# When GpSimd computes the S5 layer's second set of phases: first of its tables, or behind the last split of the first norm's output

## The chip, the cores and the metric

The kernel runs on one core of a Trainium2 chip. The core has five engines that run side by side and wait for each other by semaphores: TensorE (PE in the rows below, its weight loads PEld), VectorE (DVE), ScalarE (ACT), GpSimd (POOL) and SyncE (SP, which here only issues DMAs; ACT and POOL issue DMAs too). Every engine runs its own instructions strictly in order, so an instruction that waits holds up all that stand behind it on its engine. The metric is device time in microseconds (us); less is better.

## The reference

One block of a hybrid model on 1024 tokens and 256 context tokens, 1024 wide, in fp32: a norm with modulation, one wide projection `w_in`, two token mixers (an S5 state space layer and a gated linear attention), and a mixture of 64 experts. What matters here is the start: the first norm, the first columns of the projection (`u`, the S5 input), and the tables that S5 needs.

```python
h = rms_norm(x, lp['norm1_g']) * (1.0 + sc1) + sh1
hc = rms_norm(ctx, lp['norm1_g']) * (1.0 + csc1) + csh1
z = h @ lp['w_in']
zc = hc @ lp['w_in']
...
lam_dt = lam * dt
b_bar = ((jnp.exp(lam_dt) - 1.0) / lam)[..., None] * b
...
a = jnp.broadcast_to(jnp.exp(lam_dt), bu.shape)
_, states = lax.associative_scan(_linear_recurrence_op, (a, bu), axis=1, reverse=reverse)
```

S5 runs forward (direction 0) and backward (direction 1), with 16 groups of 64 complex states each. The kernel works in chunks of 8 tokens. Its tables are powers of `exp(lam_dt)` times B (`wts`), times C (`ca`), their product (the kernel `kts`, stored to `kd`), and the *phases*: the unit complex numbers by which a state turns in 0 to 159 chunks, one table for each direction, stored to `phd`.

## The kernel before, in words

Every fp32 product on TensorE is made of three products of fp32r halves: a tile is split into a high part (ScalarE casts or adds the shift, `hH`, `hcH`, `wH`) and the rest (VectorE subtracts, `xl`, `xcl`, `wL`; lines 127 and 295). The first norm runs over three streams: the context (stream 0, 256 columns), and two halves of the tokens (streams 1 and 2, 512 columns each), 8 row blocks each. `stats` makes the sum of squares and the inverse root (`rsqrt`, lines 89 to 93: ScalarE's root, then four small VectorE instructions), `scaled` multiplies (line 284, one operand in PSUM), `split` makes high part and rest (lines 292 and 295). The first two weight tiles (`u`) are multiplied as the splits come, in `z_step`; then `values(0)` begins, the first of the projections for the attention, in tiles of 24 products, through three PSUM buffers `z`.

The first part is written out by hand, in `tc.manual_schedule()`: there each engine's instructions stand in the order of the code. Behind it a scheduler orders `s5_tables2`, `values(0)` and what is left of direction 0's phases.

`phases(d, X)` is a generator: it builds one direction's table on engine X by doubling. A first entry 1, a second entry from `ph`, and then eight rounds (1, 2, 4, ..., 64 and 31 columns wide for 8 groups) of one complex product each: six instructions a round, lines 1233 to 1248 (`cmul_steps`), each an elementwise product or sum of two tiles in SBUF. The table lies in the buffer `big0` or `big1`, and two DMAs of GpSimd's queue store it to `phd` (line 1316). Direction 0 runs on VectorE (`V`) and is drawn step by step by the hand-written order: 24 steps (four rounds) ahead of the norm's first `rsqrt`, 3 more later, and the rest behind the last split. Direction 1 runs on GpSimd (`G`), whole, when the tables begin. Behind it GpSimd makes `ca`: for each direction six products of 128x1152 elements, and two DMAs to `cad` (line 1328). Then come GpSimd's DMAs of the first S5 input tile (`u_out(0, G)`, line 313, 8 DMAs to `ud`).

`s5_tables2` uses the buffers `big0` and `big1` again: `kts` of block 0 lies in `big0`, that of block 1 in `big1`. ScalarE copies into it from PSUM (lines 1369 and 1370) and VectorE adds 16 columns (line 1371), so both must wait until that buffer's phases are stored. `wts` of direction 0 (VectorE; its real part is whole with line 1237) is transposed on TensorE (line 1348, PSUM tile `pt`), in the middle of `values(0)`. ScalarE empties the `z` buffers of `values(0)` (line 429, `vc` and `vt`); `vt` lies where the S5 input tiles were, and waits for the `ud` DMAs too.

Of the kernel before, what the change touches and what calls it, by code (L numbers as in the profile page):

```python
# [10 lines left out]
F32 = mybir.dt.float32  # L11
# [13 lines left out]
P = 128  # L25
# [18 lines left out]
def tile_kernel(ctx: ExitStack, tc: tile.TileContext, A: dict, dbg=None):  # L44
    nc = tc.nc
    V, S, G, PE = nc.vector, nc.scalar, nc.gpsimd, nc.tensor
# [34 lines left out]
    def mm3(out, lh, ll, rh, rl, start, stop):  # L81
        PE.matmul(out, lh, rh, start=start, stop=False)  # L82
        PE.matmul(out, lh, rl, start=False, stop=False)  # L83
        return PE.matmul(out, ll, rh, start=False, stop=stop)  # L84
# [19 lines left out]
    def half(dt=F32):  # L104

        return hp.tile([P, 512], dt, name="xl", bufs=2 * KD)

    def ctx_row(dt=F32):
        return hcp.tile([P, LC], dt, name="xcl", bufs=KD + 1)
# [42 lines left out]
    def z_half(H, L, n, out=None, ks=range(KD)):  # L152
        ps = zp.tile([P, 512], F32, name="z") if out is None else out
        for k in ks:
            ws = slice(k * P, k * P + P)
            ts = slice(n * 512, n * 512 + 512)
            lastmm[0] = mm3(ps, H[:, ws], L[:, ws], hH[:, k, ts], hL[n][k], k == 0, k == KD - 1)
        return ps
# [8 lines left out]
    with tc.manual_schedule(), tc.tile_pool(name="stp", bufs=1, space=PSUM) as qp, ExitStack() as small:  # L167
        q = small.enter_context(tc.tile_pool(name="st", bufs=1))
# [50 lines left out]
        def am_steps():  # L219
# [6 lines left out]
            )  # L226

        s5t = s5_tables(nc, tc, A, cad, phd, r8d, am_steps, *s5in)
        next(s5t)
        S.activation(lg, lg, AF.Exp)  # L230
# [50 lines left out]
        def scaled(r, k):  # L281
            rows_, _, lo, hi = streams[r]
            c = 1 if r == 0 else 0
            V.scalar_tensor_tensor(
                rows_[k], rows_[k], am[:, k, c : c + 1], prs[r][:, : hi - lo], ALU.mult, ALU.mult
            )

        def split(r, k):
            rows_, H, lo, hi = streams[r]
            c, ho = (1, 0) if r == 0 else (0, lo)  # L290
            xk, Hk, sh = rows_[k], H[:, k, ho : ho + hi - lo], mod[:, k, c : c + 1]
            S.activation(Hk, xk, AF.Identity, bias=sh)  # L292
            Lk = half(F32R) if r else ctx_row(F32R)
            (hL[r - 1] if r else hcL).append(Lk)
            return V.scalar_tensor_tensor(Lk, xk, sh, Hk.bitcast(F32), ALU.add, ALU.subtract).ins  # L295

        def some(g, n):
            for _ in range(n):
                next(g, None)
# [5 lines left out]
        def u_half(m, n, ps):  # L305
            for c in range(4):

                dst = us[m][:, :, 32:160].rearrange("p j (r c) -> p c j r", c=8)[:, n * 4 + c]
                V.tensor_copy(dst, ps.rearrange("p (c j r) -> p c j r", c=4, j=8)[:, c])

        def u_out(m, E):
            for j in range(8):
                E.dma_start(ud[m].rearrange("(j c) g k -> j g c k", j=8)[j], us[m][:, j])
            dump("us%d" % m, us[m])
# [7 lines left out]
        for g in (2, 3):  # L322
            some(md[g], 3)
        s5mid = next(s5t)
        some(s5mid[3], 24)
        some(st[0], KD + 1)
        some(st[1], 4)
        some(st[0], 1)
# [5 lines left out]
        some(md[0], 1)  # L334
        some(st[1], 1)
        scaled(0, KD - 1)
        some(s5mid[3], 3)
        some(st[1], 1)
        some(md[0], 2)
        for k in range(4):  # L340
# [42 lines left out]
        for k in range(KD + 1):  # L383
            if k < KD:
                scaled(2, k)
            if k in (2, 5):
                u_half(k // 5, 0, (z00, z10)[k // 5])
            if k:
                lastL = split(2, k - 1)
        u_half(0, 1, z_half(H0, L0, 1))  # L390
        u_out(0, G)
        u_half(1, 1, z_half(H1, L1, 1))
# [6 lines left out]


    with tc.issue_after(lastL):
        some(s5mid[3], 99)
    if stop_after <= 1:
        ws_.close(); s5s.close(); early.close(); zs.close(); fr.close()
        return
# [424 lines left out]
    q = xs_.enter_context(tc.tile_pool(name="wo", bufs=1, reuse_waits="tile"))  # L830
# [261 lines left out]
def s5_tables(nc, tc, A, cad, phd, r8d, more, q, qt, par, bt, ct):  # L1092
    V, S, G, PE = nc.vector, nc.scalar, nc.gpsimd, nc.tensor
# [131 lines left out]
    def cmul_steps(or_, oi, ar_, ai, br, bi, shp, E=V, own=None):  # L1225

        n_ = int(np.prod(shp))
        t = temp(E, n_, own)
        if len(shp) == 2:
            t = t.rearrange("p (a b) -> p a b", a=shp[0])  # L1230
        if len(shp) == 3:
            t = t.rearrange("p (a b c) -> p a b c", a=shp[0], b=shp[1])
        E.tensor_tensor(or_, ar_, br, ALU.mult)
        yield
        E.tensor_tensor(t, ai, bi, ALU.mult)
        yield
        E.tensor_tensor(or_, or_, t, ALU.subtract)
        yield
        E.tensor_tensor(oi, ar_, bi, ALU.mult)
        yield  # L1240
        t2 = temp(E, n_, own)
        if len(shp) == 2:
            t2 = t2.rearrange("p (a b) -> p a b", a=shp[0])
        if len(shp) == 3:
            t2 = t2.rearrange("p (a b c) -> p a b c", a=shp[0], b=shp[1])
        E.tensor_tensor(t2, ai, br, ALU.mult)
        yield
        E.tensor_tensor(oi, oi, t2, ALU.add)
        yield

    bb = q.tile([P, 2, 16, 16], F32, name="bb")
# [7 lines left out]
    pw = q.tile([P, 2, 9, 16], F32, name="pw")  # L1259
# [29 lines left out]
    dn = q.tile([P, 2, 9, 16], F32, name="dn")  # L1289
# [8 lines left out]
    ca = q.tile([P, 2, 2, 8, 144], F32, name="ca")  # L1298
    def phases(d, X):

        big = q.tile([P, 2560], F32, name=f"big{d}")
        pt_ = big.rearrange("p (r a k) -> p r a k", r=2, a=8)
        ds_ = slice(d * 8, d * 8 + 8)
        X.memset(pt_[:, 0, :, 0:1], 1.0)
        X.memset(pt_[:, 1, :, 0:1], 0.0)
        X.tensor_copy(pt_[:, 0, :, 1], ph[:, 0, ds_])
        X.tensor_scalar(pt_[:, 1, :, 1], ph[:, 1, ds_], 1.0 - 2.0 * d, None, ALU.mult)
        n_ = 1
        while n_ < 159:
            w_ = min(n_, 159 - n_)  # L1310
            bc = lambda r: pt_[:, r, :, n_ : n_ + 1].broadcast_to([P, 8, w_])
            yield from cmul_steps(pt_[:, 0, :, n_ + 1 : n_ + 1 + w_], pt_[:, 1, :, n_ + 1 : n_ + 1 + w_],
                 pt_[:, 0, :, 1 : 1 + w_], pt_[:, 1, :, 1 : 1 + w_], bc(0), bc(1), (8, w_), E=X)
            n_ *= 2
        for r in range(2):
            G.dma_start(phd[d, r], pt_[:, r])

    for _ in phases(1, G):
        pass
    for d in range(2):  # L1320
        ps_ = slice(d * 8, d * 8 + 8)
        pwd = (pw[:, 0], pwn) if d == 0 else (dn[:, 0], dnn)
# [3 lines left out]
        cmul(cv(0), cv(1), c_(0), c_(1), g(0), g(1), (8, 9, 16), E=G)  # L1326
        for r in range(2):
            G.dma_start(cad[d, r], ca[:, d, r])
    yield q, qt, cmul, phases(0, V), bb, ca, pw, dn


def s5_tables2(nc, tc, last, lastL, A, ident, kd, wtd, qp, q, qt, cmul, phases, bb, ca, pw, dn):
# [658 lines left out]
```

## Time and profile before

| | |
|---|---|
| median of 3 runs | 2132.8 us (2128.4 to 2133.94) |
| the profiled execution's own time | 2134.74 us |
| its span, first to last instruction | 2133.1 us |
| PE busy | 1979.8 us (93%) |
| DVE, ACT, POOL busy | 1295.5, 1003.6, 485.5 us (61, 47, 23%) |
| mean granted TensorE clock | 0.976 |

The profile is of one execution: for each instruction its engine, line, start and duration, and what ended the wait before it. A busy share is a mean over the whole program; the change touches its first 150 us, which have to be read by themselves.

### The profile page before, as it was taken

Reading aid. Unit: us, or ns where it says so; the run is one execution under the profiler, and the core shown is the slowest. Engines: PE = TensorE matmul, PEld = TensorE weight load, DVE = VectorE, ACT = ScalarE, POOL = GpSimd, SP = SyncE. Lnnn points to the kernel's source line nnn. Section 1 sums busy time; section 2 is a strip of 40 time slices with the busy share of each in tenths; the row PEclk is TensorE's granted clock in tenths of the full one; section 3 lists DMA queues with packets and bytes.
Section 4 is the critical chain, followed back from the end, with each engine's and each line's share of the span. In section 5 each row is a group of like instructions: output and inputs, shape, how many; then the busy total and the mean of one; then the engine's idle time right before and its main releaser. Section 6 shows DMA issues by size and latency. Waiting matters only on the chain. (4 is left out here: it accounts for less than half of the span.)

```text
span 2133.1 us, 30727 instructions
## 1 busy us (share of the span) xinstructions
PE 1979.8 (93%) x10313; PEld 1602.0 (75%) x10313; DVE 1295.5 (61%) x2123; ACT 1003.6 (47%) x1418; POOL 485.5 (23%) x399
## 2 busy tenths in 40 slices
PE   6789999999999999997999899899999999999983
PEld 2488889888777788885877688687888887777761
DVE  7864664664577644444558667756655657776736
ACT  4334454544532411112233456756565666766631
POOL 5510000000012000001101234333333334343322
PEclk8799999999999999998999999999999999999997
DMA  8251010101144344438432699888898889998966
GB/s 310 74 142 40 24 46 31 40 31 32 49 143 158 115 134 143 134 104 302 168 131 100 254 297 306 313 266 256 260 302 247 273 261 348 334 314 248 312 159 275
DMA packets 101516, 398.73 MB, mean 187 GB/s; under 512 B 14690, under 2 KB 21474, under 8 KB 79812
## 3 DMA queue, kind: packets, MB, share of 16 engines
q1 hardware_dynamic: 60576, 260.03, 34.3%
q0 software_dynamic: 31168, 117.81, 20.8%
q10 hardware_dynamic: 9572, 18.46, 2.4%
q8 instruction: 98, 1.61, 0.3%
q14 instruction: 102, 0.84, 0.1%
HBM read 456.25 MB, written 81.55 MB: 252 GB/s over the span
## 5 line engine op out<-in xcount | busy, mean ns | idle before, releaser
L1634 DVE TENSOR_TENSOR wl<-raw,wh 128x2048 fp32r<-128x2048 f32 x156 | 352.9, 2290 | 120.2 <-ACT wh L1628 119.1
L1687 PE MATMUL pa<-wh,xh 128*128 128x512 f32 x760 | 305.3, 402 | 0.0
L1688 PE MATMUL pa<-wl,xh 128*128 128x512 f32 x760 | 299.9, 395 | 1.2 <-DVE wl L1634 0.6
L1628 ACT CAST wh<-raw 128x2048 fp32r<-128x2048 f32 x156 | 292.7, 1916 | 0.1
L83 PE MATMUL z<-xl,wH 128*128 128x512 f32 x672 | 270.6, 403 | 8.9 <-DVE xl L295 8.9
L82 PE MATMUL z<-hH,wH 128*128 128x512 f32 x672 | 268.1, 399 | 2.7 <-ACT hH L292 1.6
L84 PE MATMUL z<-hH,wL 128*128 128x512 f32 x672 | 267.0, 397 | 0.0
L1690 PE MATMUL pa<-wh,xl 128*128 128x512 f32 x496 | 193.5, 390 | 0.0
L1687 PE MATMUL py<-wh,hh 128*128 128x512 f32 x380 | 159.0, 418 | 29.4 <-ACT y L1751 19.1
L1757 POOL DMA_INDIRECT acc<-y,si x62 | 98.3, 1586 | 346.3 <-ACT y L1751 206.5
L1688 PEld LDWEIGHTS pa<-wl,xh 128*128 128x128 f32 x760 | 143.5, 189 | 34.5 <-DVE wl L1634 8.0
L1687 PEld LDWEIGHTS pa<-wh,xh 128*128 128x128 f32 x760 | 143.7, 189 | 26.4
L83 PEld LDWEIGHTS z<-xl,wH 128*128 128x128 f32 x672 | 127.4, 190 | 35.6 <-DVE xl L295 12.5
L1688 PE MATMUL py<-wl,hh 128*128 128x512 f32 x380 | 152.8, 402 | 1.2 <-DVE wl L1634 1.2
L1690 PE MATMUL py<-wh,hl 128*128 128x512 f32 x380 | 150.9, 397 | 0.0
L127 DVE TENSOR_TENSOR wL<-wraw,wH 128x1024 fp32r<-128x1024 f32 x56 | 75.0, 1346 | 121.9 <-ACT wH L122 121.8
L82 PEld LDWEIGHTS z<-hH,wH 128*128 128x128 f32 x672 | 127.3, 189 | 27.9 <-ACT hH L292 1.8
L84 PEld LDWEIGHTS z<-hH,wL 128*128 128x128 f32 x672 | 127.6, 190 | 24.5 <-issue 0.7
L1646 POOL DMA_INDIRECT xg<-h2d,gi x63 | 119.7, 1900 | 51.5 <-DVE jk L1677 17.4
L122 ACT CAST wH<-wraw 128x1024 fp32r<-128x1024 f32 x56 | 58.8, 1050 | 148.3 <-PE z L83 65.0
L1718 ACT ACTIVATE sl<-pa 128x256 f32<-128x256 f32 x95 | 36.5, 384 | 191.3 <-DVEq L1715 119.9
L1666 ACT CAST xh<-pt 128x512 fp32r<-128x512 f32 x190 | 102.1, 590 | 35.4 <-PE pt L1656 31.9
(538 smaller groups left out, 4073.9 us busy)
## 6 DMA issues: line engine op xcount, KB each, us to landing
raw<-in_wm_dram SPq DMA_DIRECT2D x285, 1024.0 KB
wraw<-in_wz_dram SPq DMA_DIRECT2D x50, 512.0 KB
wk<-in_w_ada_dram SPq DMA_DIRECT2D x64, 256.0 KB
raw<-in_wm_dram POOLq DMA_DIRECT2D x6, 1024.0 KB, 10.3
acc<-x POOLq DMA_DIRECT2D x9, 512.0 KB, 6.1
xl<-in_xcT_dram SPq DMA_DIRECT2D x16, 256.0 KB
mgd<-ga POOLq DMA_DIRECT2D x16, 256.0 KB, 3.0
xr<-in_xc_dram SPq DMA_DIRECT2D x8, 512.0 KB
```

The costliest lines, as they stand in the source:

```text
L82: PE.matmul(out, lh, rh, start=start, stop=False)
L83: PE.matmul(out, lh, rl, start=False, stop=False)
L84: return PE.matmul(out, ll, rh, start=False, stop=stop)
L127: V.tensor_tensor(L, raw, H.bitcast(F32), ALU.subtract)
L1628: S.copy(WH[b, c], raw[b % 2][c])
L1634: V.tensor_tensor(WL[b, c], raw[b % 2][c], WH[b, c].bitcast(F32), ALU.subtract)
L1646: G.indirect_dma_start(XG[b], None, h2d, IndirectOffsetOnAxis(ap=gi[:, b : b + 1], axis=0))
L1666: S.copy(xh[:, s], PX[b][hf])
L1687: PE.matmul(out, lh, rh, start=start, stop=False)
L1688: PE.matmul(out, lh, rl, start=False, stop=stop and ll is None)
L1690: PE.matmul(out, ll, rh, start=False, stop=stop)
L1757: G.indirect_dma_start(accs[b % 2], IndirectOffsetOnAxis(ap=si[:, b : b + 1], axis=0), y, None, compute_op=ALU.add)
```

## The change

Direction 1's phases are no longer run whole where the tables begin. `s5_tables` hands the generator out beside direction 0's, together with a tile `gate` of one column. The first entry of direction 1's table, which was set to 1 by GpSimd's memset, is now copied from `gate`; VectorE sets `gate` to 1 right behind the last split of stream 2. There the hand-written order also draws the whole generator, ahead of `u_out(0, G)`. So GpSimd runs the two `ca` sets first, then waits for `gate`, then runs direction 1's phases, and then the DMAs that stood behind `ca`. Direction 0's phases stay as they are.

```diff
@@ -322,7 +322,7 @@
         s5mid = next(s5t)
-        some(s5mid[3], 24)
+        some(s5mid[3][0], 24)
@@ -387,6 +387,9 @@
             if k:
                 lastL = split(2, k - 1)
+
+        V.memset(s5mid[3][2], 1.0)
+        some(s5mid[3][1], 99)
         u_half(0, 1, z_half(H0, L0, 1))
         u_out(0, G)
@@ -399,7 +402,7 @@
     with tc.issue_after(lastL):
-        some(s5mid[3], 99)
+        some(s5mid[3][0], 99)
@@ -1301,7 +1304,10 @@
         ds_ = slice(d * 8, d * 8 + 8)
-        X.memset(pt_[:, 0, :, 0:1], 1.0)
+        if d:
+            X.tensor_copy(pt_[:, 0, :, 0:1], gate.unsqueeze(1).broadcast_to([P, 8, 1]))
+        else:
+            X.memset(pt_[:, 0, :, 0:1], 1.0)
@@ -1315,8 +1321,7 @@
-    for _ in phases(1, G):
-        pass
+    gate = q.tile([P, 1], F32, name="gate")
     for d in range(2):
@@ -1326,7 +1331,7 @@
-    yield q, qt, cmul, phases(0, V), bb, ca, pw, dn
+    yield q, qt, cmul, (phases(0, V), phases(1, G), gate), bb, ca, pw, dn
```

GpSimd's order from the end of direction 1's phases (buffer `big_470`) to the DMAs of the second direction's phases (`big_561`), before:

```order
L1248 TENSOR_TENSOR big_470<-big_470,cmg 128x8x31
L1316 DMA phd<-big_470 128x1280 x2
L1233 TENSOR_TENSOR ca<-ct,pw 128x1152
...
L1328 DMA cad<-ca 128x1152 x2
L313 DMA ud<-us_951 8x16x192 x8
L1316 DMA phd<-big_561 128x1280 x2
```

And in the change, where direction 1's table is `big_928` and direction 0's `big_491` (lines from 390 on have moved down by 3 to 5):

```order
L1251 TENSOR_TENSOR ca<-ca,cmg 128x1152
L1333 DMA cad<-ca 128x1152 x2
L1308 COPY big_928<-gate 128x8
L1311 MEMSET big_928 128x8
L1312 COPY big_928<-ph 128x8
...
L1322 DMA phd<-big_928 128x1280 x2
L313 DMA ud<-us_881 8x16x192 x8
L1322 DMA phd<-big_491 128x1280 x2
```

The 52 instructions of the phases and their two DMAs have moved from ahead of the `ca` products to behind them, directly ahead of the `ud` DMAs. VectorE's order around the end of the last split, in the change:

```order
L295 SCALAR_TENSOR_TENSOR xl<-xl_106,mod,hH 128x512
L295 SCALAR_TENSOR_TENSOR xl<-xl_107,mod,hH 128x512
L391 MEMSET gate 128x1
L1242 TENSOR_TENSOR big_491<-big_491 128x8x16
L1249 TENSOR_TENSOR cmt<-big_491 128x128
```

Only the memset of `gate` is new there; the rest stands as before. ScalarE's order where it begins to fill `big1` again (`big_1236` before, `big_1238` in the change), with the semaphores that each row waits for (DMASW: DMAs of GpSimd's queue, DMAHW: those of the others), before:

```order
L122 CAST wH<-wraw 128x1024 [waits DMAHW4_49,PE_49]
L1369 COPY big_1236<-pk 16x4x128 [waits DMASW1_49,DMASW2_49,PE_49,Pool_49]
L1370 COPY big_1236<-pk 16x4x112
L429 COPY vc<-z 128x256 [waits DMAHW3_49,DMAHW2_49,DMAHW4_49,DMAHW1_49,DMAHW5_49,DMAHW0_49,DMAHW6_49,DVE_49,DMAHW7_49,PE_49,Activation_49]
L1369 COPY big_1236<-pk 16x4x128 [waits DVE_49]
```

And in the change:

```order
L122 CAST wH<-wraw 128x1024 [waits DMAHW4_49,PE_49]
L1374 COPY big_1238<-pk 16x4x128 [waits DMASW5_49,DMASW6_49,PE_49,Pool_49]
L1375 COPY big_1238<-pk 16x4x112
L1374 COPY big_1238<-pk 16x4x128 [waits DVE_49]
L1375 COPY big_1238<-pk 16x4x112
L1354 COPY wt<-pt 128x512 [waits PE_49] x2
```

The copy into `big1` still stands right behind the weight casts; the two DMAs that it waits for (DMASW5 and DMASW6 in the change) are those that store direction 1's phases, and the copies of `vc` now stand behind it and the transposed `wt`.

## Rows read from the trace of the kernel before

**Rows 1.** A stretch: us, length, busy of PE, PEld, DVE, ACT, POOL, granted clock, DMA.

```profile
46.50:84.90 38.40, 24.29 (x84) 13.21 (x77) 35.84 (x19) 14.70 (x25) 37.90 (x22) 0.67 0.31 115
```

**Rows 2.** GpSimd's timeline, 23 to 91 us: start us, duration us, line, operation.

```profile
48.88 1.20 POOL L1316 DMA_DIRECT2D phd<-big  x2
...
52.31 2.24 POOL L1235 TENSOR_TENSOR cmg<-ctn,pwn 128x1152 f32<-128x1152 f32 x1
54.63 3.53 POOL L1237 TENSOR_TENSOR ca<-ca,cmg 128x1152 f32<-128x1152 f32 x1
...
81.07 2.69 POOL L1248 TENSOR_TENSOR ca<-ca,cmg 128x1152 f32<-128x1152 f32 x1
83.70 1.13 POOL L1328 DMA_DIRECT2D cad<-ca  x2
```

**Rows 3.** VectorE's timeline: the small steps of phases, then beside GpSimd's products.

```profile
25.87 0.18 DVE L1233 TENSOR_TENSOR big<-big 128x8 f32<-128x8 f32 x1
...
30.27 0.15 DVE L90 RECIPROCAL rs_y<-rs_y 128x2 f32<-128x2 f32 x1
...
50.95 4.70 DVE L127 TENSOR_TENSOR wL<-wraw,wH 128x1024 fp32r<-128x1024 f32 x1 [2.54 <-ACT wH L122]
55.57 2.88 DVE L295 SCALAR_TENSOR_TENSOR xcl<-xcl,mod,hcH 128x256 fp32r<-128x256 f32 x1
```

**Rows 4.** VectorE's groups by line and shape, 50 to 85 us: busy, mean ns | idle.

```profile
L295 DVE SCALAR_TENSOR_TENSOR xcl<-xcl,mod,hcH 128x256 fp32r<-128x256 f32 x5 | 12.3, 2469 | 0.0
L127 DVE TENSOR_TENSOR wL<-wraw,wH 128x1024 fp32r<-128x1024 f32 x3 | 10.5, 3502 | 2.5 <-ACT wH L122 2.5
L295 DVE SCALAR_TENSOR_TENSOR xl<-xl,mod,hH 128x512 fp32r<-128x512 f32 x4 | 9.7, 2423 | 0.0
```

**Rows 5.** The same groups where GpSimd is idle, 85 to 111 and 111 to 133 us.

```profile
L295 DVE SCALAR_TENSOR_TENSOR xl<-xl,mod,hH 128x512 fp32r<-128x512 f32 x11 | 8.2, 741 | 0.4
L295 DVE SCALAR_TENSOR_TENSOR xcl<-xcl,mod,hcH 128x256 fp32r<-128x256 f32 x3 | 1.4, 476 | 2.3 <-ACT hcH L292 2.3
L127 DVE TENSOR_TENSOR wL<-wraw,wH 128x1024 fp32r<-128x1024 f32 x2 | 2.4, 1214 | 0.0
```

**Rows 6.** VectorE's timeline: the last step of the second and the third inverse root.

```profile
37.76 0.97 DVE L93 SCALAR_TENSOR_TENSOR rs_y<-rs_t,rs_y 128x4 f32<-128x4 f32 x1
...
92.75 0.16 DVE L93 SCALAR_TENSOR_TENSOR rs_y<-rs_t,rs_y 128x4 f32<-128x4 f32 x1
```

**Rows 7.** PE's timeline: first product, one z_step to the next, statistics, what follows the last.

```profile
51.75 0.56 PE L82 MATMUL prs<-hcH,wH 128*128 128x256 f32 x1
...
70.55 1.05 PE L266 MATMUL pq<-sq,ones 128*32 128x512 f32 x4
...
93.08 0.39 PE L82 MATMUL z<-hH,wH 128*128 128x512 f32 x1
...
94.14 0.39 PE L82 MATMUL z<-hH,wH 128*128 128x512 f32 x1
...
96.91 1.36 PE L279 MATMUL prs<-dg,ones 128*128 128x128 f32 x8
```

**Rows 8.** GpSimd's first step of the phases, and VectorE's last splits.

```profile
24.84 0.28 POOL L1307 TENSOR_SCALAR big<-ph 128x8 f32<-128x8 f32 x1 [0.90 <-DVE ph L1248]
...
109.61 1.62 DVE L295 SCALAR_TENSOR_TENSOR xl<-xl,mod,hH 128x512 fp32r<-128x512 f32 x2
```

**Rows 9.** VectorE's busy time behind the last split (us from:to, length, busy, clock, DMA).

```profile
111.20:131.60 20.40, 16.56 (x37) 1.00 0.56 168
```

**Rows 10.** The buffers `big`: ScalarE's copies, and their DMAs' time to landing.

```profile
L1369 ACT COPY big<-pk x4: 574/577/582, 120.9 to 137.7; 16x512 f32<-16x512 f32 x4
...
DMA to landing us min/median/max: 3.9/5.2/7.9
```

**Rows 11.** VectorE's last instruction ahead of the first transposes, and PE's wait for it.

```profile
131.64 1.22 DVE L1237 TENSOR_TENSOR wts<-wts,cmt 128x1024 f32<-128x1024 f32 x1
132.92 1.53 PE L1348 MATMUL pt<-ident,wts 128*128 128x128 f32 x8 [4.20 <-DVE wts L1237]
```

More of the change, by code (lines that the diff above doesn't have):

```diff
@@ L336, in tile_kernel @@
         scaled(0, KD - 1)
-        some(s5mid[3], 3)
+        some(s5mid[3][0], 3)
         some(st[1], 1)
```

## The prediction

> **What bounds the kernel now.** TensorE is busy for 93% of the span, so first I looked for where it isn't: in the first 133 us. I read the stretch table there, then the timelines of GpSimd, VectorE and TensorE side by side. From 46.5 to 84.9 us TensorE works for 24.3 of 38.4 us at a granted clock of 0.67 (mostly its lower level, 1.2 GHz), while VectorE shows 35.8 us busy and GpSimd 37.9 [rows 1]. VectorE's busy time there is mostly no work. An `xcl` split that takes 0.48 us where GpSimd is idle takes 2.47 in the mean, a `wL` 3.50 for 1.21, an `xl` split 2.42 for 0.74 [rows 4, 5]. Over the three groups that is (12.3 - 2.4) + (10.5 - 3.6) + (9.7 - 3.0) = 23.5 us of waiting. The timelines show for what: the `wL` that starts at 50.95 ends at 55.65, 1.1 us behind the end of GpSimd's second product (52.31 + 2.24 = 54.55), and the `xcl` behind it ends at 58.45, just when the next product has ended (54.63 + 3.53 = 58.16) [rows 2, 3]. So a VectorE instruction with both operands in SBUF waits until GpSimd's running product ends, about one gets in between two products, and the product behind it is stretched (3.53 us for 2.69) [rows 2]. GpSimd's `ca` products are therefore on the path of the first z_steps, which wait for VectorE's splits.
>
> **The change, step by step.** *The products move forward.* GpSimd's first work in the change is `ca`. Its first product needs `pw`, which stands ahead of VectorE's small phase steps (25.87) [rows 3], so it can start at about 25. Eight products of 2.24 us, four of 2.69 and two DMA issues of 1.13 make 31.0 us unhindered; before, they took from 50.08 to 84.83, 34.75 us [rows 2]. So VectorE pushed them back by 3.8 us. VectorE's steps are now shorter, so I take 33 us: the products end at 58, with 56 and 60 as bounds.
>
> *What they now lie beside.* Not the splits, but direction 0's 24 small steps, which stand on VectorE ahead of the norm's first root. They took 25.87 to 30.27 [rows 3], 0.18 us each, because GpSimd's own steps were as small as they. Now each meets a product of 2.2 to 2.7 us. With one or two let in at a boundary, the first set of six products admits some 6 steps, the DMA issue behind it (1.13 us) some 6 to 8 more at their old pace, the second set 6, and the rest run when the products are over. The root then starts at 58, not at 30.27: 27.7 us later. Bounds: 42 us, if all are through by the first DMA issue (25 + 16 + 1), and 60. I take 58, since one instruction in about each gap is what the ten blocked ones of rows 3 and 4 did.
>
> *What is won behind it.* From that root to the last split (109.61 + 1.62 = 111.2) before took 81.0 us [rows 3, 8]. Then GpSimd is idle, waiting for `gate`. The roots get some 2 us shorter (one step took 0.97 us for 0.16 [rows 6]; four such). The z_step loop took from 51.75 to 96.91, 45.2 us. Left to TensorE it needs 16 steps at 1.06 us (93.08 to 94.14), four groups of statistics at 1.05, and some 3 us for the start at the lower clock and the rest: 24.5 us [rows 7]. VectorE's own work in the loop (8 splits of both kinds, 4 scalings like a split, 3 `wL`) is 8 x 1.22 + 4 x 0.74 + 3 x 1.21 = 16.4 us and hides under it [rows 5]. So 20.7 us are won there, 22.7 in all, and the last split ends at 58 + 81.0 - 22.7 = 116.3, 5.1 us later than before. The gain of taking the products off the splits is more than paid for by the small steps.
>
> *The phases at their new place.* They took from 24.84 to 48.88, 24 us [rows 2, 8]; with the copy from `gate` and the two instructions behind it, 25. Beside them VectorE now has all that it did from 111.2 to 131.6, 16.6 us [rows 9]. How much of that pushes GpSimd back? In the product stretch ten VectorE instructions of 3 x 1.21 + 4 x 0.48 + 3 x 0.74 = 7.8 us pushed it by 3.8, so 0.48 of their time. 0.48 x 16.6 = 8 us. Bounds: nothing, and the whole 16.6. The phases end at 116.3 + 25 + 8 = 149.3.
>
> *Who waits for them.* The order shows ScalarE's copy into `big1` waiting for the two DMAs that store this table, directly behind the weight casts, and in order: behind it stand `wt`, `vc` and `vt`, which free TensorE's `z` buffers. VectorE's `L1371` waits for that copy, and `wts` (line 1237 of before) stands behind it. TensorE's first transpose waits for that `wts`; it did already, for 4.2 us, at 132.92 [rows 11]. Then that ended VectorE's own queue; now the chain is: one DMA issue 0.6 (half of 1.20), landing of the second 5.2, two copies of at most 0.58 each, VectorE's small addition and `wts` (0.3 + 1.22): 8.5 us behind the phases' end [rows 2, 10, 11]. The transpose starts at 149.3 + 8.5 = 157.8, 24.9 us later than at 132.92. TensorE, three `z` tiles ahead, has nothing else to do meanwhile.
>
> *What I cost at nothing.* The `gate` memset is one instruction of VectorE's queue; behind it stand direction 0's steps, which wait for nothing new. The `ud` DMAs come behind the phases' DMAs: six can be issued at once (0.6 us each, as those of the phases), the last two reuse the lanes of the phases' DMAs and wait for their landing, so with 5.2 us of their own they land some 12 us behind the phases' end. `vt` waits for them, but ScalarE comes to `vt` only behind the transposes and `wt`, 8.5 + 1.5 + 1.5 us, about then; if they are later, each us is one more. Stores to `kd`, `wtd` and `phd` shift by as much; they are read behind the attention.
>
> *Sum.* -2 - 20.7 + 27.7 = +5.0 to the last split, +19.8 from there to the transpose (41.5 for 21.7), 24.9 with rounding. TensorE is the bound behind it, so the end shifts alike: 2134.7 + 24.9 = 2159.6 for the profiled execution, which lay 1.9 above the median of its runs; 2158 against that median. Something under 0.3% (6.4 us) can't be told from no change here.
>
> **The rivals.** *Small steps slip through (2148).* If several pass at each gap and all are done by 42, the last split ends at 42 + 81.0 - 20.7, with some 4 us for the roots now beside products: 106.3. The rest, 41.5 us, puts the transpose at 147.8, 14.9 late. For it: where a product needs the one before, the gap may take two steps. Against: long VectorE instructions got one gap each.
>
> *Strict exclusion (2166).* GpSimd's phases lose the whole of VectorE's 16.6 us, not 8: the transpose is 33.5 us late. The step of 4.70 us that sat out two products [rows 3] speaks for it, the stretch of 3.8 for 7.8 us against. The Trainium skill, page "SBUF — State Buffer", section "Who interferes with whom", states that a VectorE instruction with two SBUF inputs and a GpSimd instruction that reads SBUF exclude each other, and whoever starts first holds the port for its whole instruction. By that rule, the time is this rival's; the trace agrees that the loser waits, but not that all of its time is added, as 3.8 of 7.8 us shows.
>
> *The other sign: the products cost the small steps nothing (2124).* Then the root stays at 30.3, the loop is free of GpSimd from the start, the last split ends at 111.2 - 20.7 = 90.5, the phases are unhindered (25), and the transpose starts at 90.5 + 25 + 8.5 = 124, 8.9 early. It decides for faster from a last split ahead of 93. For it: the 24 steps did well beside GpSimd before. Against: those GpSimd steps were ten times shorter.
>
> *Nothing in sum (2133).* Between these: the root at about 35, with a wait for the table that is as long as the start is shorter. That the change doesn't do what it says can be left out: the order shows the phases behind the copy from `gate`, and GpSimd works in order.
>
> **How the numbers follow.** Forecast 62%, slipping through 16%, strict exclusion 12%, nothing in sum 6%, the other sign 4%. The first three are slower: 90%; same 6%, faster 4%. The forecast's bounds (56 to 60 for the root, some 4 us either way for the pushing back) give 2150 to 2164; the range, 2143 to 2168, takes in slipping through and strict exclusion and leaves out the other two.
>
> **What would show it.** Right: VectorE's small steps spread over 26 to 58 us with durations up to 2.7; the first root near 58; z_steps then without waits for VectorE; the last split near 116; GpSimd's phases lasting over 30 us; ScalarE idle ahead of the `big1` copy, released by the `phd` DMA; TensorE's first transpose near 158 after a wait of some 24 us. Wrong: a root well ahead of 50, which takes the first half of the loss away; or TensorE finding work past the transpose.

## The result, and the profile after

2156.0 us (median of 3 runs, 2155.1 to 2160.7) for 2132.8 before: 1.0115 of the time, 95% interval 1.0099 to 1.0131. Slower, as forecast, and 2 us below the forecast of 2158. The profiled execution took 2155.1 us with a span of 2153.5, so 20.4 more than the profiled one of before in both.

GpSimd's timeline of the changed kernel (columns as in [rows 2]; the bracket is the idle time ahead and what ended it):

```profile
23.02 2.37 POOL L1236 TENSOR_TENSOR ca<-ct,pw 128x1152 f32<-128x1152 f32 x1 [20.79 <-DVE pw L1240]
27.08 2.28 POOL L1238 TENSOR_TENSOR cmg<-ctn,pwn 128x1152 f32<-128x1152 f32 x1 [1.69 <-DVE pwn L1298]
...
54.54 1.13 POOL L1333 DMA_DIRECT2D cad<-ca  x2
110.53 0.20 POOL L1308 COPY big<-gate 128x8 f32<-128x8 f32 x1 [54.86 <-DVE gate L391]
...
143.11 1.17 POOL L1322 DMA_DIRECT2D phd<-big  x2
```

The products now run from 23.0 to 55.7 and the phases from 110.5 to 143.1. VectorE's timeline shows what each of them does to it:

```profile
29.63 2.47 DVE L1240 TENSOR_TENSOR big<-big,cmt 128x8 f32<-128x8 f32 x1
32.02 0.16 DVE L1242 TENSOR_TENSOR big<-big 128x8 f32<-128x8 f32 x1
32.14 2.18 DVE L1249 TENSOR_TENSOR cmt<-big 128x8 f32<-128x8 f32 x1
34.35 2.17 DVE L1251 TENSOR_TENSOR big<-big,cmt 128x8 f32<-128x8 f32 x1
...
39.71 5.12 DVE L1238 TENSOR_TENSOR cmt<-big 128x32 f32<-128x32 f32 x1
...
55.38 0.16 DVE L90 RECIPROCAL rs_y<-rs_y 128x2 f32<-128x2 f32 x1
...
108.81 1.62 DVE L295 SCALAR_TENSOR_TENSOR xl<-xl,mod,hH 128x512 fp32r<-128x512 f32 x2
...
150.59 0.21 DVE L1376 TENSOR_TENSOR big<-big,pk 16x64 f32<-16x64 f32 x1 [21.21 <-ACT big L1375]
150.74 1.21 DVE L1240 TENSOR_TENSOR wts<-wts,cmt 128x1024 f32<-128x1024 f32 x1
```

The small steps that took 0.18 us [rows 3] take 2.2 to 2.7 beside a product, with up to two of 0.2 between; the one at 39.71 sat out two products. The first root stands at 55.4 instead of 30.3. From there VectorE runs free until the last split ends at 110.4 (111.2 before); from 129.4 on it sits idle for 21 us ahead of its small addition into `big1`. ScalarE's row says for what, and TensorE's rows what comes of it:

```profile
149.04 0.57 ACT L1374 COPY big<-pk 16x512 f32<-16x512 f32 x1 [31.36 <-DMA phd<-big]
```

```profile
72.49 0.39 PE L82 MATMUL prs<-hcH,wH 128*128 128x256 f32 x1
...
96.14 1.36 PE L279 MATMUL prs<-dg,ones 128*128 128x128 f32 x8
...
152.00 1.97 PE L1353 MATMUL pt<-ident,wts 128*128 128x128 f32 x8 [24.07 <-DVE wts L1240]
```

The z_step loop, 72.5 to 96.1, takes 23.65 us for 45.2 [rows 7], and the first transpose starts at 152.0 for 132.92 [rows 11]. TensorE's list of waits from 0 to 200 us (in total, times, longest) holds nothing else of that size behind the root's 27.8:

```profile
PE prs L279 <- ACT dg L278: 27.8, 1, 27.8
PE pt L1353 <- DVE wts L1240: 24.1, 1, 24.1
```

So the start came out even (the late root was paid for by a free loop), and the loss lies behind the last split. To see that in every run I use one landmark more: the first transpose of the attention (tile `pkt`), 200.3 us before and here

```profile
L591 PE MATMUL pkt<-ident,tm x96: 270/272/329, 221.0 to 618.0; 128*128 128x128 f32 x96
```

The 96 of them last 397 us in every kernel, so nearly all of the differences have arisen ahead of the first. All times in this table but the ratio are us of the one profiled execution:

| kernel | first root | last split ends | from there to `pkt` | `pkt` | ratio to before, 95% interval |
|---|---|---|---|---|---|
| before | 30.3 | 111.2 | 89.1 | 200.3 | 1 |
| the change | 55.4 | 110.4 | 110.6 | 221.0 | 1.0115 (1.0099 to 1.0131) |
| x1_nogate | 55.9 | 114.0 | 90.8 | 204.8 | 1.0025 (1.0016 to 1.0035) |
| x4_late24 | 28.4 | 95.7 | 106.4 | 202.1 | 1.0006 (0.9996 to 1.0016) |
| x5_oneset | 41.9 | 99.4 | 110.5 | 209.9 | 1.0044 (1.0030 to 1.0058) |
| x2b_short | 57.7 | 114.2 | 100.4 | 214.6 | 1.0062 (1.0044 to 1.0080) |
| x6_nogate_late24 | 27.8 | 94.4 | 84.6 | 179.0 | 0.9902 (0.9886 to 0.9918) |
| x7_gateca | 30.3 | 90.7 | 121.2 | 211.9 | 1.0061 (1.0044 to 1.0078) |
| x8_before_late24 | 28.8 | 103.4 | 84.7 | 188.1 | 0.9935 (0.9919 to 0.9951) |
| x9_d0short | 55.0 | 110.1 | 111.1 | 221.2 | 1.0106 (1.0089 to 1.0122) |
| x10_twelve | 39.3 | 100.5 | 108.7 | 209.2 | 1.0072 (1.0048 to 1.0097) |

(x2b_short's profiled execution began its first product 2.3 us later than the change's, at 25.35; its root is late by as much, its last split by 3.8.)

### The profile page after: what moved, and what is told of

The parts are those of the page before. It is cut to its first block, busy times and chain, and to the rows that moved or that the text cites. A ratio compares the mean times of both kernels' runs of the same rounds, so it can differ in the third digit from the quotient of the medians.

```text
span 2153.5 us, 30728 instructions
## 1 busy us (share of the span) xinstructions
PE 1982.4 (92%) x10313; PEld 1605.6 (75%) x10313; DVE 1296.1 (60%) x2124; ACT 1003.9 (47%) x1418; POOL 496.9 (23%) x399
## 5 line engine op out<-in xcount | busy, mean ns | idle before, releaser
L1692 PE MATMUL py<-wh,hh 128*128 128x512 f32 x380 | 159.4, 419 | 28.2 <-ACT y L1756 17.1
L83 PEld LDWEIGHTS z<-xl,wH 128*128 128x128 f32 x672 | 126.8, 189 | 27.8 <-DVE xl L295 4.8
L84 PEld LDWEIGHTS z<-hH,wL 128*128 128x128 f32 x672 | 127.0, 189 | 24.5 <-issue 0.7
L127 DVE TENSOR_TENSOR wL<-wraw,wH 128x1024 fp32r<-128x1024 f32 x56 | 68.4, 1228 | 122.8 <-ACT wH L122 122.7
```

The costliest lines, as they stand in the source:

```text
L127: V.tensor_tensor(L, raw, H.bitcast(F32), ALU.subtract)
```

## The experiments

All edits are against the changed kernel, but for x8.

**Without the gate** (x1_nogate). The phases run directly behind the products.

```diff
-        V.memset(s5mid[3][2], 1.0)
-        some(s5mid[3][1], 99)
...
-        if d:
-            X.tensor_copy(pt_[:, 0, :, 0:1], gate.unsqueeze(1).broadcast_to([P, 8, 1]))
-        else:
-            X.memset(pt_[:, 0, :, 0:1], 1.0)
+        X.memset(pt_[:, 0, :, 0:1], 1.0)
...
+    for _ in phases(1, G):
+        pass
```

> The change without the gate: GpSimd runs the two ca sets first, and direction 1's phases directly behind them, from about 56 us on, beside the z_steps instead of behind the last split. Theory (all of the loss is TensorE's wait at the first transposes for the phases that end at 143): the first root stays at about 55, the phases end at 56 + 25 to 30 = 81 to 86, the last split comes at 110 to 115 (some 0 to 4 us of pushing beside the z_steps), the transpose 22 us behind it, at 132 to 137, so the time is 2133 to 2138, no more than 0.3% over the kernel before. Rival (the late root and the reordered start are the loss, the wait only absorbs slack): 2150 to 2156. Second rival (the phases beside the z_steps stretch VectorE's splits as the products did before, by 20 us): last split at 130, 2152.

Measured 1.0025, inside the 0.3% that was expected (2139.6 us, where before took 2134.8 beside it): most of the loss is gone. The phases are stored from 83.25, and TensorE's wait at the transposes is 3.4 us instead of 24.1:

```profile
PE pt L1349 <- DVE wts L1238: 3.4, 1, 3.4
```

The late root is still there, at 55.9. The last split is 3.6 us later than in the change, within what was expected of phases beside the z_steps; against before, 2.8 us are left at the last split and 1.7 behind it. Both rivals fall.

**A shorter second table** (x2b_short).

```diff
+            X.memset(pt_[:, :, :, 65:160], 0.5)
...
-        while n_ < 159:
+        while n_ < (64 if d else 159):
```

> The change with the last two rounds of direction 1's phases left out (64 and 31 columns wide, twelve instructions that took 10.5 us behind the last split; their columns are set to 0.5 by one memset of GpSimd ahead of the copy from the gate, in its idle time, so that this table is not computed there). Theory (TensorE's wait at the transposes ends with this table, stored): the phases end at 132.6, TensorE waits 13 to 14 us instead of 24, and the time is 10 to 11 us below the change: 2144.5 to 2146. Rival (VectorE's or ScalarE's other work behind the last split would hold the transposes anyway): 2150 to 2156.

Measured 1.0062, 0.53% or 11.3 us below the change's 1.0115, where 10 to 11 were expected (the 2148.7 us themselves lie above the 2144.5 to 2146), and the wait for `wts` falls by 9.3 us:

```profile
PE pt L1354 <- DVE wts L1240: 14.8, 1, 14.8
```

GpSimd's phases last 20.4 us (114.31 to 134.74) instead of 32.6, so 12.2 less. ScalarE's copy into `big1` starts 5.9 us behind their end in both kernels and comes 12.2 us earlier too. The transposes gain only 9.1 of that, counted from the last split, and `pkt` 10.2. The rest went to VectorE's queue: its `wts` stands 0.15 us behind the small addition in the change (150.59, 150.74) and 3.5 here (141.88, 145.40), because the scheduler put five of direction 0's steps and one more instruction between them. So the phases hold the transposes, as the theory has it, and the rival is right for some 3 of the 12 us.

**One set of products** (x5_oneset).

```diff
-        cmul(cv(0), cv(1), c_(0), c_(1), g(0), g(1), (8, 9, 16), E=G)
+        if d == 0:
+            cmul(cv(0), cv(1), c_(0), c_(1), g(0), g(1), (8, 9, 16), E=G)
+        else:
+            for r in range(2):
+                G.memset(ca[:, d, r], 0.5)
```

> The change with direction 1's six ca products left out (that half of ca is set to 0.5 by two memsets of GpSimd, so that half of the kernel table is not computed). Theory (about one small step per gap, so the steps last until the products end): GpSimd's products end near 40, the steps that are left then run at 0.18 us each, the first root starts at 41 to 44 instead of 55.4, all behind it shifts alike, the phases end at 129 to 132, and the time is 11 to 14 us below the change: 2142 to 2145. Rival (the products do not set the root): 2154 to 2157.

Root at 41.9, phases' end at 132.1, 2143.8 us, all where they were expected. The products set the root.

**Twelve steps instead of 24** (x10_twelve).

```diff
-        some(s5mid[3][0], 24)
+        some(s5mid[3][0], 12)
...
-        some(s5mid[3][0], 3)
```

> The change with 12 of direction 0's small steps ahead of the first root instead of 24 (and without the 3 steps behind them): how many products does a step have to wait for? Theory (a small step gets through only at the ends of products, one to three at each): twelve steps are through at the end of the first set of ca, at 39 to 40, so the first root starts at 39.5 to 41.5, between 28.4 with none and 55.4 with 24. The roots' own steps then meet the second set until 56. Last split at 98 to 103 (95.7 with none, 110.4 with 24), the wait for the phases as in the change, so the time is 1.003 to 1.007 of the kernel before. Rival (the steps are not served at the products' ends, but the first of them waits for all products): root at 55, ratio 1.010 to 1.012.

1.0072 lies just above the 1.003 to 1.007 that were expected, and its interval ends at 1.0097, just short of the rival's 1.010; the place of the root parts the two clearly. VectorE's timeline:

```profile
39.24 0.19 DVE L1250 TENSOR_TENSOR big<-big,cmt 128x16 f32<-128x16 f32 x1
39.34 0.15 DVE L90 RECIPROCAL rs_y<-rs_y 128x2 f32<-128x2 f32 x1
39.60 0.16 DVE L91 SCALAR_TENSOR_TENSOR rs_t<-z,rs_y 128x2 f32<-128x2 f32 x1
39.79 4.75 DVE L92 SCALAR_TENSOR_TENSOR rs_t<-rs_t,rs_y 128x2 f32<-128x2 f32 x1
...
46.49 2.83 DVE L284 SCALAR_TENSOR_TENSOR xcl<-xcl,am,prs 128x256 f32<-128x256 f32 x7 [1.75 <-PE prs L279]
```

Twelve steps are through at 39.4, in the gap that the DMA issues (38.90 to 40.07) leave between the two sets. The next instruction with two tiles in SBUF sits out two products. The seven scalings at 46.49, which read one tile in SBUF and one in PSUM (`prs`), take 0.40 us each beside running products: they don't wait. That agrees with the Trainium skill, page "SBUF — State Buffer", section "Who interferes with whom", which says that a VectorE instruction with at most one SBUF input does not contend with GpSimd, as long as it is outside the 2-port perf modes.

**The small steps behind the last split** (x4_late24).

```diff
-        some(s5mid[3][0], 24)
...
-        some(s5mid[3][0], 3)
```

> The change with direction 0's 24 small steps (and the 3 steps behind them) taken from ahead of the norm's roots; they run behind the last split with the rest of direction 0. Theory (the steps hold the root until the products end): the root starts at 26 to 29 instead of 55.4. But now the norm's own VectorE instructions meet the products until 56, one in a gap, so the first z_step comes at about 57 instead of 72.5, the last split at 95 to 98 instead of 110.4, the phases end at 129 to 133, and the time is 11 to 15 us below the change: 2141 to 2145. Rival (VectorE is not what sets the start; the loads of the norm's input or TensorE at its lower clock are): last split within 3 us of 110, time 2153 to 2157. Second rival (the products hold the norm's longer instructions as much as they held the small steps): 2150.

The root (28.4) and the last split (95.7) are where they were expected. The time is not: 2136.6 us, level with before, where 2141 to 2145 was expected. Two more terms moved. The phases last 30.4 us (95.80 to 126.21) instead of 32.6, and the scheduler now puts more of `values(0)` ahead of the transposes (237 instructions of TensorE from the last split on, for 206 in the change), so that TensorE waits at another place, for a `z` buffer, behind the same copy of ScalarE:

```profile
PE z L82 <- ACT vc L430: 21.3, 1, 21.3
```

The wait for the phases is still 21 us. It moves with its table, not with the instruction that happens to stand first behind it.

**Both away** (x6_nogate_late24): the edits of x1 and x4 together.

> Both parts of the loss taken away: the products first and the phases directly behind them without the gate, and direction 0's 27 small steps behind the last split. Theory (the wait for the phases was the whole loss, and the early products leave the z_steps nearly free): last split at 95.7, as without the small steps alone, and 3.6 later for the phases beside the z_steps, 99; no wait for big1; the transposes 22 us behind it and some 5 more for the small steps that now stand there, 126 instead of 132.9 before, so the time is 5 to 9 us below the kernel before, a ratio of 0.996 to 0.998. Rival (what is won ahead of the last split is lost behind it on VectorE, where direction 0's steps are 27 more): ratio 0.999 to 1.003.

0.9902: 1.0% faster than before, the best kernel of this study, and some 14 us more than I had expected. Two steps of the expectation failed. The last split ends at 94.4, not 99: the phases beside the z_steps cost 0.3 us here (it is 1.3 us earlier than in x4, where the products ended 1.6 later). And the 27 steps behind it cost nothing that shows: 84.6 us to the landmark, 4.5 less than before. The scheduler puts more of `values(0)` ahead of the transposes here too, and TensorE is busy for 24.3 of the 25.4 us from the last split to the first of them (17.5 of 21.7 before). TensorE's largest waits from 20 to 200 us are now one for a `wL`, from the stretch in which products still run (until 55.8), and five for `xl` splits, which add up to 4.9:

```profile
PE prs L84 <- DVE wL L127: 5.8, 1, 5.8
PE z L83 <- DVE xl L295: 4.9, 5, 1.8
```

**The small steps alone, in the kernel before** (x8_before_late24; the same two lines removed from the kernel before).

> The kernel before with direction 0's 24 and 3 small steps moved behind the last split, and nothing else. Theory (the early steps cost little where GpSimd's own steps are small: 4.4 us ahead of the root): the root starts at 26 instead of 30.3, the z_steps still run beside the products until 85, so the last split gains 0 to 4 us and the steps cost 4 to 5 behind it: ratio 0.999 to 1.002. Rival (the small steps as such hold the start, also without products beside them): ratio below 0.997.

0.9935, a miss: the rival was right that these steps cost something without products beside them. Not through the root, though, which comes only 1.5 us earlier, since it then waits for ScalarE:

```profile
28.75 0.17 DVE L90 RECIPROCAL rs_y<-rs_y 128x2 f32<-128x2 f32 x1 [3.45 <-ACT rs_y L89]
```

The first product of the z_steps starts at 45.89 instead of 51.75 [rows 7]. Of these 5.9 us, 3.3 are TensorE's clock: from the first product for `mod` to the z_steps it takes 4.56 us at a granted clock of 1.00, and 7.87 at 0.50 before. The z_steps so start ahead of GpSimd's products (51.03), and four splits and two `wL` get through before these begin, where before it was two splits and no `wL`; the last split is 7.9 us earlier. Behind it 4.4 us more are won. The steps stand ahead of `wts` there, but the scheduler has put more of `values(0)` in front of the transposes (TensorE runs 240 instructions from the last split to the first transpose, for 206 before), and its wait for `wts`, 4.2 us before [rows 11], is 1.1.

**The other order** (x7_gateca). Direction 1's phases first, as before; the products behind the gate.

```diff
-        if d:
-            X.tensor_copy(pt_[:, 0, :, 0:1], gate.unsqueeze(1).broadcast_to([P, 8, 1]))
-        else:
-            X.memset(pt_[:, 0, :, 0:1], 1.0)
+        X.memset(pt_[:, 0, :, 0:1], 1.0)
...
+    for _ in phases(1, G):
+        pass
+
+    def tables():
+        G.tensor_copy(ca[:, 0, 0, 0, 0:1], gate)
+        for d in range(2):
...
-    yield q, qt, cmul, (phases(0, V), phases(1, G), gate), bb, ca, pw, dn
+    yield q, qt, cmul, (phases(0, V), tables(), gate), bb, ca, pw, dn
```

> The other order: direction 1's phases first, as before, and the ca products behind the gate. Theory (products beside the splits cost the z_steps some 20 us, and nothing but the loop's own work is left there): last split at 90 to 92 instead of 111; then the twelve products run from 91 to 126 or 130 beside VectorE's wts, each of which waits for a product. The wts and the copies of the kernel table come late by 8 to 13 us, so the time is 7 to 12 us below the kernel before, a ratio of 0.994 to 0.997. Rival (the products behind the gate hold TensorE or the copies into the kernel table, as the phases did in the change): ratio 1.002 to 1.008.

The first half came out (last split at 90.7, the earliest of all), the second didn't: 1.0061, inside the rival's range. The products behind the gate did hold TensorE, not by the copies but through VectorE's queue: the steps of direction 0 that are left there now meet products, and the `wL` that TensorE needs stands behind them. VectorE's rows, and TensorE's wait:

```profile
99.69 2.49 DVE L1242 TENSOR_TENSOR big<-big 128x256 f32<-128x256 f32 x1
102.09 2.47 DVE L1240 TENSOR_TENSOR big<-big,cmt 128x256 f32<-128x256 f32 x1
...
108.03 4.82 DVE L1249 TENSOR_TENSOR cmt<-big 128x256 f32<-128x256 f32 x1
...
118.17 3.26 DVE L127 TENSOR_TENSOR wL<-wraw,wH 128x1024 fp32r<-128x1024 f32 x1
```

```profile
PE z L83 <- DVE wL L127: 18.8, 1, 18.8
```

**Less VectorE work beside the phases** (x9_d0short).

```diff
-        while n_ < 159:
+        while n_ < (159 if d else 64):
...
+        if d == 0:
+            V.memset(pt_[:, :, :, 65:160], 0.5)
```

> The change with the last two rounds of direction 0's phases left out (VectorE's twelve instructions of 0.5 to 0.9 us from 116.4 to 127.8; one memset of VectorE sets their columns to 0.5, so that this table is not computed there). It takes some 7 us of VectorE's work from beside GpSimd's phases behind the last split. Theory (VectorE's work pushes GpSimd back by about half of its time): direction 1's phases last 29 us instead of 32.6, and the time is 3 to 4 us below the change, a ratio to the kernel before of 1.0095 to 1.0105 for 1.0115. Rival (strict exclusion: all of VectorE's time is added): 26 us and 6 to 7 us less, 1.008 to 1.0085. Second rival (what stretches GpSimd's steps is not VectorE): 32 to 33 us, 1.011 to 1.012.

1.0106, with an interval that takes in the theory's ratio and the second rival's, but not the first rival's of 1.0085. The phases' own time speaks: 110.15 to 144.40 less two DMA issues of 0.6 us that the order put between them is 33.0 us, no shorter than 32.6. Not all of the 7 us of VectorE's work are gone, though: a memset of 1.3 us and three more instructions for `wts` stand beside the phases instead, and VectorE is busy there for 16.0 us, for 18.5 in the change. Half of that 2.5 would still have made the phases 1.3 us shorter, and strict exclusion 2.5. x4 says it more plainly: there VectorE is busy for 25.0 us beside the phases, more than in the change, and they take 30.4, which is less. So neither "half of VectorE's time" nor all of it holds. What counts is which instruction stands beside which. In x9 `wts` and `wL` instructions moved up beside GpSimd's steps of 128x64, which take 0.30 to 0.32 us in x1. GpSimd's rows, then VectorE's:

```profile
119.16 1.28 POOL L1238 TENSOR_TENSOR cmg<-big 128x64 f32<-128x64 f32 x1
120.52 1.18 POOL L1240 TENSOR_TENSOR big<-big,cmg 128x64 f32<-128x64 f32 x1
121.66 1.29 POOL L1242 TENSOR_TENSOR big<-big 128x64 f32<-128x64 f32 x1
```

```profile
118.96 1.32 DVE L1238 TENSOR_TENSOR cmt<-dn,bb 128x1024 f32<-128x1024 f32 x1
120.20 1.32 DVE L127 TENSOR_TENSOR wL<-wraw,wH 128x1024 fp32r<-128x1024 f32 x1
121.44 1.34 DVE L1240 TENSOR_TENSOR wts<-wts,cmt 128x1024 f32<-128x1024 f32 x1
```

Each of these GpSimd steps ends 0.16 to 0.18 us behind a VectorE instruction, one for one, so a short GpSimd step takes as long as the long VectorE instruction that it meets (1.18 to 1.29 for 0.31), while VectorE loses only 0.1 of 1.22.

## Why the prediction was right

The case that I forecast is the one that happened: the small steps hold the root until the products end, the loop behind is free of GpSimd, the phases become late for `big1`, and TensorE waits for them. x5 and x10 show the first link, x1 and x2b the last. That the medians lie only 2 us from the forecast is partly luck: the two profiled executions differ by 20.4 us where I forecast 24.9, and before's median in 20 later runs was 2134.8, not 2132.8. The sum, step by step:

| step | forecast | measured |
|---|---|---|
| products end | 58 (56 to 60) | 55.7 |
| first root | 58 | 55.4 |
| root to the first product of the z_steps | 19.5 (21.5 less 2) | 17.1 |
| z_step loop | 24.5 | 23.65 |
| last split ends | 116.3 | 110.4 |
| phases behind it | 33 | 32.6 |
| phases' end to the transpose | 8.5 | 8.9 |
| the transpose against before | +24.9 | +19.1 |
| the span | +24.9 | +20.4 |

- **The products' end was mis-sized by 2.3 us.** I let VectorE push the products back by 2. It did not: 32.7 us less the 1.7 of waiting for `pwn` is the 31.0 of the unhindered sum, so this wait happens to stand in for the push. The error is the start, which I had at 25; the real part of `pw` alone releases the first one at 23.0, in the midst of VectorE's chain for the rest, which it then holds up (that is the wait of 1.7).
- **The stretch from the root to the z_steps was mis-sized by 2.4 us.** It became 4.4 us shorter, not 2. Up to the first product for `mod` (`pm`) it is 1.05 us (13.61 before, 12.56 now): VectorE's steps of the second root and direction 0's three steps behind it had been stretched by GpSimd's phases, as I priced for the root; the scalings had not (2.83 us for seven in both kernels). The other 3.3 us are TensorE's clock, for which I had no term: from there to the first z_step it took 7.87 us at a granted clock of 0.50 before, its lower level, behind a wait of 2.1 us for `dg`; in the change it takes 4.55 at 1.00, without that wait. The same eight products, before and after:

```profile
43.88 1.87 PE L255 MATMUL pm<-sel,mr 128*128 128x2 f32 x8 [0.70 <-ACT mr L253]
```

```profile
67.94 1.05 PE L255 MATMUL pm<-sel,mr 128*128 128x2 f32 x8 [0.70 <-ACT mr L253]
```

  GpSimd's work there does not decide it: with its phases or products beside it this stretch is at 1.00 in x1, x6 and x8 and at 0.50 in x4 and x7.
- **The loop was over by 0.85 us.** I had added some 3 us for a start at the lower clock; it ran at a granted clock of 1.00 throughout (0.74 before). The terms as I gave them make 24.2, not 24.5. In all 5.9 us at the last split, which is the forecast's error up to the transpose.
- **The phases and the chain behind them** were right to 0.4 us each, but 33 was right by luck: the rule behind it is disproved by x4 and x9, and GpSimd's loss of 7.6 us was a matter of which instructions met.
- **Behind the transposes 1.3 us more were lost.** TensorE had stood still since 128. It took up work again at its lower level: the granted clock of the first 15 us is 0.81, for 0.88 in the first 14 of before, and the first eight transposes take 1.97 us for 1.53 [rows 11]. I had no term for that; how much of the 1.3 us the clock makes isn't separated. These are the stretches of the changed kernel (columns as in [rows 1]):

```profile
130.00:152.00 22.00, 0.00 (x1) 0.01 (x1) 1.36 (x3) 2.20 (x4) 19.73 (x28) 0.51 0.30 94
...
151.95:167.00 15.05, 15.00 (x101) 14.41 (x102) 10.01 (x11) 7.04 (x16) 0.87 (x3) 0.81 0.61 201
```

What I had put at nothing in the change's own edits did cost nothing that shows: seven of the `ud` DMAs are issued at once (I had six), the eighth waits 0.7 us, and `vt` doesn't wait for them.

Of the rivals, "slipping through" had the root at 42; that takes half of the steps (x10) or of the products (x5). The other sign, with the last split at 90.5, needed the steps out of the way. With them gone (x4) the split comes at 95.7, and the wait for the phases still eats what that wins. Strict exclusion needed phases of 41.6 us; 32.6 were measured. So the change holds a gain that it doesn't collect, as the ratios show when they are laid out by its parts:

| GpSimd's order | small steps early | small steps late |
|---|---|---|
| phases, products (before) | 1 | 0.9935 |
| products, phases | 1.0025 | 0.9902 |
| products, phases behind the gate (the change) | 1.0115 | 1.0006 |

The gate costs 0.9 to 1.0% in either column. Products first costs 0.25% with the early steps beside them and gains 0.33% without. The early steps cost 0.65 to 1.2% in every row; no part of the change touched them, and I took their place as given. The phases beside the z_steps delay the last split by some 3 us with the early steps (x1) and by 0.3 without (x6). The rows show where: in x1 the widest phase steps (69 to 83 us) lie beside the first splits, which follow each other without a pause, and all of the delay is there by the first statistics in the loop (80.6 for 77.0). In x6 they lie at 75 to 86, when the splits of this loop are through (74.7). No run moves the phases alone to test this.

## What to carry to other kernels

When long GpSimd work is moved, look for the short VectorE instructions that it will now lie beside: each can cost the length of a GpSimd instruction, and a row of them ahead of a root that TensorE waits for can eat all that the freed splits win. Work that is moved to a place where "nobody needs it yet" has to be followed through its buffer: here the next user of `big1` stood 10 us behind the new place (120.9 for 111.2 before [rows 8, 10]) while the phases last 33, and everything of ScalarE and VectorE behind it in order. Read a wait by what it waits for, not by the instruction that shows it; x4 moved it from the transposes to a `z` buffer, and 21 of its 24 us stayed.

## What the runs showed of the hardware

- A VectorE instruction with both operands in SBUF got in at the end of GpSimd's running product, with up to two short ones behind it, but not always: one that came while the first product of a set ran sat out two products, 5.12 us in the change and 4.75 in x10, as 4.70 in [rows 3]. What lets the others in isn't settled by these runs.
- Short VectorE steps cost GpSimd's long products nothing (31.0 us for 31.0), while long VectorE instructions stretch GpSimd's short steps to their own length (1.28 us for 0.31 in x9). In both, the shorter of the two paid. It isn't always the only one: in the kernel before, the product behind the `wL` that had waited for two took 3.53 us for 2.69 [rows 2, 3].
- A one-input instruction can wait too: VectorE's `TENSOR_SCALAR` on 8 columns took 2.23 us beside a product in the change:

```profile
27.16 2.23 DVE L1313 TENSOR_SCALAR big<-ph 128x8 f32<-128x8 f32 x1
```
